# Spreading the modulation slabs of two later layers over both products of the second MLP

## The chip, the cores and the metric

One Trainium2 chip, one core of it. A time is the device time of one execution in microseconds (us), the median of several runs. The kernel before takes 2263.5 us (three runs: 2257.25, 2263.5 and 2268.2).

## The reference, cut to what matters

Four layers, each a token mixer (Hyena, gated linear attention, latent attention, Hyena) and then a squared-ReLU MLP, over 256 latent and 256 context tokens of width 1024. Every sub-layer is modulated by six vectors ("maps": shift, scale and gate, twice) that one linear map per layer makes from the condition vectors.

```python
for i in range(DEPTH):                       # 4 layers
    mod_l = split(silu(c)     @ ada_w[i] + ada_b[i], 6)     # six maps, latent tokens
    mod_c = split(silu(c_ctx) @ ada_w[i] + ada_b[i], 6)     # the same, context tokens
    x_lat = x_lat + mod_l[2] * mixer(modulate(rmsnorm(x_lat), mod_l[0], mod_l[1]))
    h = modulate(rmsnorm(x_lat), mod_l[3], mod_l[4])
    x_lat = x_lat + mod_l[5] * (square(relu(h @ mlp_w1[i])) @ mlp_w2[i])
    # the context tokens likewise, with mod_c, as long as a later layer reads them
```

`ada_w[i]` is 1024 x 6144 in f32, `mlp_w1[i]` 1024 x 4096, `mlp_w2[i]` 4096 x 1024. The maps of layers 2 and 3 depend on the condition vectors alone, so they can be made at any time before those layers.

## The kernel before, in words

Matrix products run on TensorE (PE) as three passes of a split operand: weights and activations are each cut into a high and a low part, and `mm3` (L369 to L371) multiplies high by high, high by low and low by high. A weight tile of 512 KB is loaded by SyncE's DMA queue (SP) into `wraw` (5 buffers), rounded by ScalarE (ACT) into `wh` (L359, 4 buffers), and GpSimd (POOL) makes the rest `wl` (L360, 4 buffers).

**The second MLP** (`mlp`, layer 1, 512 tokens) is the place of the change. `hidden(c)` makes 128 hidden units for all tokens: 24 matmuls of 512 columns into a bank `mm` (two banks; `cv` for two of the first four), then on ACT the ReLU (L645), on VectorE (DVE) the square (L646), on ACT the high part `fH` (L176) and on DVE the low part `fL` (L177). There are 32 of them. `residual` is the second product: for each group of four hidden blocks, 8 output tiles, each 12 matmuls of 512 columns into one of three `cv` banks, and after each tile two DVE additions into `x` (L600, one per 256 tokens). A `cv` bank is free for the next tile when these two are done. The loop over 8 groups makes the first hidden block of the next group, then the 8 tiles of this group, then the other three hidden blocks of the next group.

**The maps of layers 2 and 3** are made beside this MLP, by the generator `ada_lone`. There are 12 maps, each of 8 slabs of `ada_w` (128 x 1024, 512 KB, tag `adaw`, three buffers, named `lw` here), so 96 slabs, loaded on the same SP queue as the weights. DVE multiplies a slab by one element of the condition vector per partition and adds: two instructions of 128 x 512 per slab into two PSUM tiles `st` (L434 for the first slab, L436 after). Two of the 12 maps (layer 2, q = 0 and 1, third and fourth in order) are also wanted for the context tokens and take a third instruction of 128 x 1024 per slab into an SBUF tile `la` (L440, L442). After the eighth slab the sums over the partitions follow: four or eight small matmuls with ones on PE (L449, into the bank `ada`), a 32 x 32 transpose on DVE (L388) and the bias (L391, L394) in `ada_part`.

**What sets the order.** A scheduler orders each engine's instructions by priority of the program's order and by its own times; each engine then runs its list in that order. `more()` lets slabs out after each of 28 hidden blocks, at 96/26 = 3.69 slabs a block and none in the tiles; `issue_after(behind())` lets a slab's DVE work issue only after the low part of the latest hidden block (`last[0]`). The last slab of a map and its sums over the partitions are one step of the generator.

Of the kernel before, what the change touches and what calls it, by code (L numbers as in the profile page):

```python
# [15 lines left out]
ALU = mybir.AluOpType  # L16
# [4 lines left out]
KD = D // P  # L21
# [106 lines left out]
def trunk_kernel(ctx: ExitStack, tc: tile.TileContext, ins: dict, table, zpos, out, layers=(0, 1, 2, 3)):  # L128
    nc = tc.nc
# [11 lines left out]
    def nm(s):  # L141
        seq[0] += 1
        return f"{s}_{seq[0]}"
# [5 lines left out]
    def bank(tag="mm"):  # L149
        if tag in turns:  # L150

            turns[tag] += 1
            if turns[tag] % (banks[tag] + 1) == 0:
                tag = "ada"
        return pp.tile([P, 512], F32, tag=tag, name=nm(tag), bufs=banks[tag])
# [85 lines left out]
    def scratch(n, shape, dt=F32):  # L241
        return up.tile(shape, dt, tag=f"uL{n}", name=nm("scr"))
# [3 lines left out]
    for b in range(8):  # L246
        src = g["x"] if b < 4 else g["ctx"]
        t = up.tile([P, 512], F32, tag=f"uH{b}", name=nm("xr"))
        r0, c0 = (b % 4) // 2 * P, b % 2 * 512
# [37 lines left out]
    if need_hy:  # L287
# [10 lines left out]
        for q, w in enumerate((w1, w2)):  # L298
            ps = bank()
# [6 lines left out]
        ps = bank()  # L306
# [7 lines left out]
        r = scratch(1, [P, 2, SEQ], F32R)  # L314
# [9 lines left out]
    xT = [cp.tile([P, TOK], F32, tag=f"x{k}", name=f"x{k}") for k in range(KD)]  # L324
    for k in range(KD):
        ps = bank("cv")
# [41 lines left out]
    def mm3(ps, lh, ll, rh, rl, start, stop):  # L368
        nc.tensor.matmul(ps, lh, rh, start=start, stop=False)  # L369
        nc.tensor.matmul(ps, lh, rl, start=False, stop=False)  # L370
        nc.tensor.matmul(ps, ll, rh, start=False, stop=stop)  # L371


    mods = {}
# [8 lines left out]
    def ada_part(i, q, ps, s):  # L383

        m, a = ada_maps(i)
        n = s.stop - s.start
        tr = np_.tile([P, KD, 32], F32, tag="adatr", name=nm("adatr"), bufs=1)
        nc.vector.transpose(tr.rearrange("p t c -> p (t c)"), ps)  # L388
        o = pcol[("ada_b", 0 if i < 2 else 2)] + (i % 2) * 48 + q * KD
        bias = params[:, o : o + KD].unsqueeze(2).broadcast_to([P, KD, n])  # L390
        nc.vector.tensor_tensor(m[:, q, :, s], tr[:, :, :n], bias, ALU.add)  # L391
        if q in (1, 4):
            gn = pcs("norm1_g" if q == 1 else "norm2_g", i * KD, KD).unsqueeze(2).broadcast_to([P, KD, n])
            nc.vector.scalar_tensor_tensor(a[:, q // 4, :, s], m[:, q, :, s], 1.0, gn, ALU.add, ALU.mult)  # L394
# [22 lines left out]
    def ada_lone(parts, mp, behind):  # L417

        hd = D // 2
        for i, q, n in parts:

            run = [bank("st") for _ in range(2)]
            acc = [mp.tile([P, D], F32, tag=f"la{r}", name=nm("la"), bufs=1) for r in range(n)]
            for k in range(KD):
                wt = wp.tile([P, D], F32, tag="adaw", name=nm("lw"), bufs=3)
                nc.sync.dma_start(wt, g["ada_w"][i, k * P : (k + 1) * P, q * D : (q + 1) * D])
                with tc.issue_after(behind()):
                    for b in range(2):  # L430
                        cols = slice(b * hd, (b + 1) * hd)
                        dst = acc[0][:, cols] if k == KD - 1 else run[b]
                        if k == 0:
                            nc.vector.tensor_scalar(dst, wt[:, cols], sT[:, k, 0:1], None, ALU.mult)  # L434
                        else:
                            nc.vector.scalar_tensor_tensor(dst, wt[:, cols], sT[:, k, 0:1], run[b], ALU.mult, ALU.add)  # L436
                    for r in range(1, n):
                        c = sT[:, k, r : r + 1]
                        if k == 0:
                            nc.vector.tensor_scalar(acc[r], wt, c, None, ALU.mult)  # L440
                        else:
                            nc.vector.scalar_tensor_tensor(acc[r], wt, c, acc[r], ALU.mult, ALU.add)  # L442
                if k < KD - 1:
                    yield
            ps = bank("ada")
            for r in range(n):
                av = acc[r].rearrange("p (t j c) -> p j t c", j=4, c=32)
                for j in range(4):
                    nc.tensor.matmul(ps[32 * j : 32 * j + 32, r * 256 : (r + 1) * 256], ones[:, :32], av[:, j],  # L449
                                     start=True, stop=True, tile_position=(0, 32 * j))  # L450
            for r in range(n):
                ada_part(i, q, ps[:, r * 256 : (r + 1) * 256], slice(r, r + 1) if n == 2 else slice(0, 2))
            yield

    ada_q = []

# [3 lines left out]
    def pump(n, keep=0):  # L460

        while n > 0 and ada_q and ada_q[0][1] > ada_q[0][2][keep]:
            next(ada_q[0][0], None)
            ada_q[0][1] -= 1
            n -= 1
            if ada_q[0][1] == 0:
                next(ada_q.pop(0)[0], None)
# [110 lines left out]
                mm3(ps[:, s], wh[:, k, :m], wl[:, k, :m], uH[k][:, s], uL[k][:, s],  # L578
                    k == 0 and n == 0, k == KD - 1 and n == len(parts) - 1)

    def residual(i, gi, wmat, r0, fH, fL, nt, tag="mm", halves=False):

        nk = len(fH)
        parts = [slice(r * SEQ, (r + 1) * SEQ) for r in range(nt // SEQ)] if halves else [slice(0, nt)]

        def slabs(c):
            return [wload(wmat[r0 + p * 2 * P : r0 + (p + 1) * 2 * P, c * 512 : (c + 1) * 512]
                          .rearrange("(k p) c -> p k c", p=P), [P, 2, 512]) for p in range(nk // 2)]

        def columns(c, w, s):  # L590
            for d in range(4):
                ps = bank(tag)
                for k in range(nk):
                    wh, wl = w[k // 2]
                    mm3(ps[:, s], wh[:, k % 2, d * P : (d + 1) * P], wl[:, k % 2, d * P : (d + 1) * P],
                        fH[k][:, s], fL[k][:, s], k == 0, k == nk - 1)
                dt = c * 4 + d
                for r in range(s.start // SEQ, s.stop // SEQ):
                    q = slice(r * SEQ, (r + 1) * SEQ)
                    nc.vector.scalar_tensor_tensor(xT[dt][:, q], ps[:, q], mods[i][:, gi, dt, r : r + 1],  # L600
                                                   xT[dt][:, q], ALU.mult, ALU.add)

        if nk == 2 or halves:
            w = [slabs(0), slabs(1)]
            for s in parts:
                if s.start > 0:
                    last_part.append(tc.cur_priority)
                for c in range(2):
                    columns(c, w[c], s)
        else:  # L610
            for c in range(2):
                columns(c, slabs(c), parts[0])


    def mlp(i, nt, later=None, lone=()):
# [3 lines left out]
        with ExitStack() as es:  # L619
# [3 lines left out]
            if later is not None:  # L623
                fp = es.enter_context(tc.tile_pool(name=nm("fs"), bufs=1))
                later = filters(later, fp, dft_table(fp, "dftt", fp, "w4r"), "st", True)
            last = [None]
            extra = ada_lone(lone, mp, lambda: last[0])

            def hidden(c):
# [23 lines left out]
            groups = HID // 512  # L653
# [23 lines left out]
                                                               ALU.mult, ALU.add)  # L677

            fs = [hidden(c) for c in range(4)]
            count = [0]  # L680

            def more():
                count[0] += KD * len(lone)
                while count[0] >= 4 * groups - 6:
                    count[0] -= 4 * groups - 6
                    next(extra, None)

            for grp in range(groups):
                if later is not None:
                    for _ in range(2 if grp == 0 else 1):  # L690
                        next(later, None)

                nxt = []
                if grp + 1 < groups:
                    nxt.append(hidden(4 * grp + 4))
                    more()
                if single:
                    accumulate(grp)
                else:
                    residual(i, 5, g["mlp_w2"][i], grp * 512, [f[0] for f in fs], [f[1] for f in fs], nt, "cv",  # L700
                             halves=grp == groups - 1)
                if grp + 1 < groups:
                    for q in range(1, 4):
                        nxt.append(hidden(4 * grp + 4 + q))
                        more()
                        pump(1, 16)
                fs = nxt
                pump(2, 16)

    def together(chains):  # L710

        while chains:
            chains = [c for c in chains if next(c, chains) is not chains]
# [762 lines left out]
    lone = []  # L1476
    if len(layers) == DEPTH:
        lone = [(2, q, 2 if q < 2 else 1) for q in (3, 4, 0, 1, 2, 5)] + [(3, q, 1) for q in range(6)]
# [5 lines left out]
    for li, i in enumerate(layers):  # L1484
        kind, j = i % 3, i // 3
        both = any(l % 3 != 0 for l in layers[li + 1 :])
        nt = TOK if both else SEQ
# [71 lines left out]
```

## Time and profile before

| | before |
|---|---|
| median of three runs | 2263.5 us (2257.25 to 2268.2) |
| profiled execution | 2267.3 us, its span 2265.5 us |
| PE busy, share of the span | 2096.4 us, 93% |
| DVE busy | 1345.5 us, 59% |
| POOL busy | 1118.0 us, 49% |
| ACT busy | 905.7 us, 40% |
| DMA, mean | 145 GB/s |

PE is the engine with the most work, and for most of the span its line in the profile's 40 slices is at 9 (90% or more busy). The slices of the second MLP are those from about 1140 to 1510 us; several of them show PE at 8 or 7 and the DMA share at its highest since the start. Matmuls are pipelined: a matmul's shown duration is longer than its share of the engine's time, so the pitch from one start to the next is what counts.

### The profile page before, as it was taken

What the parts mean: (1) busy time and instruction counts of PE and PEld (TensorE: products, weight loads), DVE (VectorE), ACT (ScalarE), POOL (GpSimd) and SP (SyncE); (2) the same over time, 40 slices, a digit from 0 to 9 for tenths busy, and PEclk for the clock granted to TensorE, in tenths of its full rate; (3) what the DMA queues carried; (4) which work ended last, traced back from release to release, by engine and by line L of the source; (5) the groups of instructions that cost most, each with busy time, mean ns of one, the idle gap of its engine ahead of it and who ended that gap; (6) DMA issues with size and microseconds to landing.
All of it is one profiled execution on the core that took longest, in us unless ns stands there. A gap on an engine that the chain in (4) does not pass through costs nothing. (4 is left out here: it accounts for less than half of the span.)

```text
span 2265.5 us, 33310 instructions
## 1 busy us (share of the span) xinstructions
PE 2096.4 (93%) x12834; PEld 1781.8 (79%) x12834; DVE 1345.5 (59%) x2412; ACT 905.7 (40%) x1505; POOL 1118.0 (49%) x669
## 2 busy tenths in 40 slices
PE   6998999899999999998899988898989997887998
PEld 3766687777888889876777767687779997887998
DVE  7855887764344354455747976668673227996223
ACT  2642333343333234444432222236445445544444
POOL 5653444256544443322243333334347886674886
PEclk7998999999999999999999999999999997998999
DMA  9666635533333332212137677733135564433663
GB/s 313 185 211 222 206 112 177 167 96 117 110 105 99 107 88 74 67 57 65 47 117 246 211 253 227 244 115 109 66 116 164 180 190 131 126 115 94 182 191 112
DMA packets 322301, 329.12 MB, mean 145 GB/s; under 512 B 21276, under 2 KB 248673, under 8 KB 322143
## 3 DMA queue, kind: packets, MB, share of 16 engines
q1 hardware_dynamic: 321012, 326.05, 46.3%
q8 instruction: 101, 1.65, 0.3%
q10 hardware_dynamic: 587, 0.61, 0.1%
q14 instruction: 57, 0.47, 0.1%
q0 software_dynamic: 544, 0.34, 0.1%
HBM read 317.51 MB, written 9.44 MB: 144 GB/s over the span
## 5 line engine op out<-in xcount | busy, mean ns | idle before, releaser
L360 POOL TENSOR_TENSOR wl<-wraw,wh 128x1024 fp32r<-128x1024 f32 (+2 forms) x378 | 908.0, 2416 | 944.9 <-ACT wh L359 887.4
L359 ACT CAST wh<-wraw 128x1024 fp32r<-128x1024 f32 (+2 forms) x378 | 390.3, 1041 | 615.7 <-PE mm L370 229.4
L370 PE MATMUL mm<-uL,wh 128*128 128x512 f32 (+3 forms) x1288 | 455.1, 354 | 14.1 <-DVE uL L531 8.7
L369 PE MATMUL mm<-uH,wh 128*128 128x512 f32 (+3 forms) x1288 | 454.0, 356 | 14.5 <-DVE zb L568 5.4
L371 PE MATMUL mm<-uH,wl 128*128 128x512 f32 (+3 forms) x1288 | 451.5, 352 | 0.0
L369 PEld LDWEIGHTS mm<-uH,wh 128*128 128x128 f32 (+1 forms) x1288 | 249.6, 195 | 56.6 <-issue 15.1
L370 PEld LDWEIGHTS mm<-uL,wh 128*128 128x128 f32 (+1 forms) x1288 | 251.0, 195 | 49.3 <-DVE uL L531 13.1
L371 PEld LDWEIGHTS mm<-uH,wl 128*128 128x128 f32 (+1 forms) x1288 | 251.3, 195 | 32.5 <-issue 3.0
L369 PE MATMUL cv<-fH,wh 128*128 128x512 f32 (+1 forms) x576 | 213.3, 377 | 28.6 <-DVE x L600 21.3
L370 PE MATMUL cv<-fL,wh 128*128 128x512 f32 (+1 forms) x576 | 213.5, 373 | 0.7 <-DVE fL L177 0.6
L371 PE MATMUL cv<-fH,wl 128*128 128x512 f32 (+1 forms) x576 | 212.4, 372 | 0.0
L600 DVE SCALAR_TENSOR_TENSOR x<-cv,mods,x 128x256 f32<-128x256 f32 x256 | 112.1, 477 | 114.0 <-PE cv L371 113.8
L369 PEld LDWEIGHTS cv<-fH,wh 128*128 128x128 f32 x576 | 110.4, 193 | 52.0 <-issue 25.1
L370 PE MATMUL sum<-fL,wh 128*128 128x256 f32 x512 | 138.5, 278 | 0.0
L369 PE MATMUL sum<-fH,wh 128*128 128x256 f32 x512 | 137.0, 278 | 0.0
L371 PE MATMUL sum<-fH,wl 128*128 128x256 f32 x512 | 136.8, 278 | 0.0
L370 PEld LDWEIGHTS cv<-fL,wh 128*128 128x128 f32 x576 | 111.0, 193 | 20.4 <-issue 1.3
L371 PEld LDWEIGHTS cv<-fH,wl 128*128 128x128 f32 x576 | 110.5, 192 | 19.0 <-issue 0.7
L369 PE MATMUL mm<-oH,wh 128*128 128x256 f32 (+1 forms) x288 | 102.6, 358 | 23.5 <-DVE x L600 18.0
L646 DVE SCALAR_TENSOR_TENSOR mm<-mm,r 128x512 f32<-128x512 f32 x60 | 41.6, 694 | 130.1 <-ACT r L645 130.1
L436 DVE SCALAR_TENSOR_TENSOR st<-lw,sT,st 128x512 f32<-128x512 f32 x144 | 101.5, 747 | 22.3 <-DMA lw<-in_ada_w_dram 22.2
L565 DVE COPY rbias<-st 128x1 f32<-128x1 f32 x32 | 5.1, 158 | 163.5 <-PE st L371 163.5
(479 smaller groups left out, 4565.4 us busy)
## 6 DMA issues: line engine op xcount, KB each, us to landing
wraw<-in_mlp_w_dram SPq DMA_DIRECT2D x256, 512.0 KB
adaw<-in_ada_w_dram SPq DMA_DIRECT2D x96, 512.0 KB
lw<-in_ada_w_dram SPq DMA_DIRECT2D x96, 512.0 KB
wraw<-in_hy_w_in_dram SPq DMA_DIRECT2D x48, 512.0 KB
wraw<-in_gla_w_in_dram SPq DMA_DIRECT2D x24, 512.0 KB
spec<-S SPq DMA_DIRECT2D x16, 512.0 KB
wraw<-in_hy_w_out_dram SPq DMA_DIRECT2D x16, 512.0 KB
S<-spec SPq DMA_DIRECT2D x32, 256.0 KB
```

What stands on the lines that cost most here:

```text
L359: nc.scalar.copy(wh[r0:r1, :n], raw[r0:r1, :n])
L360: nc.gpsimd.tensor_tensor(wl[r0:r1, :n], raw[r0:r1, :n], rounded(wh[r0:r1, :n]), ALU.subtract)
L369: nc.tensor.matmul(ps, lh, rh, start=start, stop=False)
L370: nc.tensor.matmul(ps, lh, rl, start=False, stop=False)
L371: nc.tensor.matmul(ps, ll, rh, start=False, stop=stop)
L436: nc.vector.scalar_tensor_tensor(dst, wt[:, cols], sT[:, k, 0:1], run[b], ALU.mult, ALU.add)
L565: nc.vector.tensor_copy(bias, ps[:, SEQ : SEQ + 1])
L600: nc.vector.scalar_tensor_tensor(xT[dt][:, q], ps[:, q], mods[i][:, gi, dt, r : r + 1], xT[dt][:, q], ALU.mult, ALU.add)
L646: nc.vector.scalar_tensor_tensor(r, r, 0.0, pos, ALU.max, ALU.mult)
```

## The change

Slabs are let out after every piece of matmul work in proportion to its matmuls: `more(24)` after a hidden block, and `more(12)` after each tile of `residual` in the first seven groups, through the new argument `each`. With `total` = 7 x (4 x 24 + 8 x 12) - 24 = 1320, a hidden block lets out 96 x 24/1320 = 1.745 slabs and a tile 0.873. After a tile, `last[0]` is the tile's second addition, so the slab's DVE work is put behind that. The generator now yields after every slab, the eighth too, and the sums over the partitions of a map are made at the start of its next step, which then goes on to the first slab of the next map; a last loop finishes the twelfth map. The computation is the same.

```diff
@@ ada_lone, end of the loop over the slabs
-                if k < KD - 1:
-                    yield
+                yield
+
             ps = bank("ada")
...
                 ada_part(i, q, ps[:, r * 256 : (r + 1) * 256], slice(r, r + 1) if n == 2 else slice(0, 2))
-            yield
@@ residual
-                    nc.vector.scalar_tensor_tensor(xT[dt][:, q], ps[:, q], mods[i][:, gi, dt, r : r + 1],
-                                                   xT[dt][:, q], ALU.mult, ALU.add)
+                    add = nc.vector.scalar_tensor_tensor(xT[dt][:, q], ps[:, q], mods[i][:, gi, dt, r : r + 1],
+                                                         xT[dt][:, q], ALU.mult, ALU.add)
+                if each is not None:
+                    each(add.ins)
@@ mlp
-            count = [0]
-
-            def more():
-                count[0] += KD * len(lone)
-                while count[0] >= 4 * groups - 6:
-                    count[0] -= 4 * groups - 6
+
+            total, count = (groups - 1) * (4 * 24 + 8 * 12) - 24, [0]
+
+            def more(matmuls):
+                count[0] += KD * len(lone) * matmuls
+                while count[0] >= total:
+                    count[0] -= total
                     next(extra, None)
+
+            def after_tile(ins):
+                last[0] = ins
+                more(12)
...
-                    more()
+                    more(24)
...
                     residual(i, 5, g["mlp_w2"][i], grp * 512, [f[0] for f in fs], [f[1] for f in fs], nt, "cv",
-                             halves=grp == groups - 1)
+                             halves=grp == groups - 1,
+                             each=after_tile if lone and grp + 1 < groups else None)
...
-                        more()
+                        more(24)
...
+            for _ in extra:
+                pass
```

**How the order moves, place 1.** DVE in the sixth group, from the end of the middle one of three hidden blocks in a row to the first tile's addition (`mm` and `fL` belong to a hidden block, `lw`, `st` and `la` to a map, `cv` and `x` to a tile). Before:

```order
L436 SCALAR_TENSOR_TENSOR st_12002<-lw_12062,sT,st_12002 128x512
L177 TENSOR_TENSOR fL_12101<-mm_12073,fH_12100 128x512
L436 SCALAR_TENSOR_TENSOR st_12001<-lw_12104,sT,st_12001 128x512
L436 SCALAR_TENSOR_TENSOR st_12002<-lw_12104,sT,st_12002 128x512
L436 SCALAR_TENSOR_TENSOR la_12003<-lw_12108,sT,st_12001 128x512
L436 SCALAR_TENSOR_TENSOR la_12003<-lw_12108,sT,st_12002 128x512
L646 SCALAR_TENSOR_TENSOR mm_12134<-mm_12134,r_12133 128x512
L434 TENSOR_SCALAR st_12120<-lw_12123,sT 128x512
L434 TENSOR_SCALAR st_12121<-lw_12123,sT 128x512
L177 TENSOR_TENSOR fL_12162<-mm_12134,fH_12161 128x512
L600 SCALAR_TENSOR_TENSOR x_179<-cv_12193,mods_5225,x_179 128x256 x2
```

The same place of the change (L648 is L646 of before):

```order
L177 TENSOR_TENSOR fL_12093<-mm_12065,fH_12092 128x512
L436 SCALAR_TENSOR_TENSOR st_12001<-lw_12096,sT,st_12001 128x512
L436 SCALAR_TENSOR_TENSOR st_12002<-lw_12096,sT,st_12002 128x512
L648 SCALAR_TENSOR_TENSOR mm_12107<-mm_12107,r_12106 128x512
L177 TENSOR_TENSOR fL_12135<-mm_12107,fH_12134 128x512
L436 SCALAR_TENSOR_TENSOR st_12001<-lw_12138,sT,st_12001 128x512
L436 SCALAR_TENSOR_TENSOR st_12002<-lw_12138,sT,st_12002 128x512
L600 SCALAR_TENSOR_TENSOR x_179<-cv_12158,mods_5225,x_179 128x256 x2
L600 SCALAR_TENSOR_TENSOR x_180<-cv_12177,mods_5225,x_180 128x256 x2
L436 SCALAR_TENSOR_TENSOR st_12001<-lw_12142,sT,st_12001 128x512
L436 SCALAR_TENSOR_TENSOR st_12002<-lw_12142,sT,st_12002 128x512
```

One slab instead of two or more stands between two hidden blocks, and the slabs go on between the tiles' additions.

**Place 2.** DVE among the tiles of the second group, where the first map with a third instruction (`la` of 128 x 1024) runs, in the change:

```order
L600 SCALAR_TENSOR_TENSOR x_183<-cv_10739,mods_5225,x_183 128x256 x2
L442 SCALAR_TENSOR_TENSOR la_10681<-lw_10702,sT,la_10681 128x1024
L434 TENSOR_SCALAR st_10679<-lw_10682,sT 128x512
L436 SCALAR_TENSOR_TENSOR st_10678<-lw_10702,sT,st_10678 128x512
L600 SCALAR_TENSOR_TENSOR x_184<-cv_10759,mods_5225,x_184 128x256 x2
L442 SCALAR_TENSOR_TENSOR la_10681<-lw_10722,sT,la_10681 128x1024
L436 SCALAR_TENSOR_TENSOR st_10679<-lw_10702,sT,st_10679 128x512
L436 SCALAR_TENSOR_TENSOR st_10678<-lw_10722,sT,st_10678 128x512
L388 STREAM_TRANSPOSE adatr_10674<-ada_10669 128x256
L442 SCALAR_TENSOR_TENSOR la_10681<-lw_10754,sT,la_10681 128x1024
L600 SCALAR_TENSOR_TENSOR x_185<-cv_10774,mods_5225,x_185 128x256 x2
```

Before, one L442 stood between two additions here, and the next six came behind hidden blocks.

**Place 3.** The SP queue at the start of the second group (`wraw` is a weight, `lw` a slab). Before:

```order
L358 DMA wraw_10650<-in_mlp_w_dram 128x2x512
L428 DMA lw_10448<-in_ada_w_dram 128x1024
L428 DMA lw_10452<-in_ada_w_dram 128x1024
L428 DMA lw_10456<-in_ada_w_dram 128x1024
L358 DMA wraw_10656<-in_mlp_w_dram 128x2x512
L358 DMA wraw_10722<-in_mlp_w_dram 128x2x512
L358 DMA wraw_10728<-in_mlp_w_dram 128x2x512
L358 DMA wraw_10794<-in_mlp_w_dram 128x8x128
L358 DMA wraw_10852<-in_mlp_w_dram 128x8x128
L428 DMA lw_10460<-in_ada_w_dram 128x1024
```

And in the change:

```order
L358 DMA wraw_10623<-in_mlp_w_dram 128x2x512
L428 DMA lw_10323<-in_ada_w_dram 128x1024
L428 DMA lw_10342<-in_ada_w_dram 128x1024
L428 DMA lw_10373<-in_ada_w_dram 128x1024
L428 DMA lw_10407<-in_ada_w_dram 128x1024
L358 DMA wraw_10629<-in_mlp_w_dram 128x2x512
L428 DMA lw_10426<-in_ada_w_dram 128x1024
L358 DMA wraw_10727<-in_mlp_w_dram 128x2x512
L428 DMA lw_10481<-in_ada_w_dram 128x1024
L428 DMA lw_10485<-in_ada_w_dram 128x1024
L358 DMA wraw_10733<-in_mlp_w_dram 128x2x512
```

The slab loads now stand between the weight loads of the tiles too, one or two behind each. Everything ahead of the second MLP's first tile stands in the same order as before; behind this MLP the lists differ in a few short stretches of the last layer.

## Rows read from the trace of the kernel before

**Rows 1.** Busy time of each engine from the first slab to the last.

```profile
1160.00:1508.00 348.00, 319.68 (x1437) 254.90 (x1440) 246.52 (x403) 86.05 (x108) 130.54 (x57) 0.96 0.69 222
```

**Rows 2.** PE's timeline: idle of over 1 us between 1160 and 1508.

```profile
1211.82 0.47 PE L369 MATMUL cv<-fH,wh 128*128 128x512 f32 x1 [3.21 <-DVE x L600]
...
1261.64 0.77 PE L369 MATMUL cv<-fH,wh 128*128 128x512 f32 x1 [3.46 <-DVE x L600]
...
1310.86 0.64 PE L449 MATMUL ada<-la,ones 128*32 128x256 f32 x8 [1.13 <-DVE la L436]
1316.58 0.76 PE L369 MATMUL cv<-fH,wh 128*128 128x512 f32 x1 [5.09 <-DVE x L600]
...
1370.78 0.77 PE L369 MATMUL cv<-fH,wh 128*128 128x512 f32 x1 [5.93 <-DVE x L600]
...
1421.24 0.47 PE L369 MATMUL cv<-fH,wh 128*128 128x512 f32 x1 [3.62 <-DVE x L600]
...
1472.10 1.08 PE L449 MATMUL ada<-la,ones 128*32 128x256 f32 x8 [4.65 <-DVE la L436]
```

**Rows 3.** PE's timeline behind the stalls at 1316 and 1370.

```profile
1317.14 0.63 PE L370 MATMUL cv<-fL,wh 128*128 128x512 f32 x1
...
1322.26 0.60 PE L370 MATMUL cv<-fL,wh 128*128 128x512 f32 x1
...
1323.18 0.39 PE L370 MATMUL cv<-fL,wh 128*128 128x512 f32 x1
...
1327.52 0.39 PE L371 MATMUL cv<-fH,wl 128*128 128x512 f32 x1
...
1373.48 0.59 PE L369 MATMUL cv<-fH,wh 128*128 128x512 f32 x1
```

**Rows 4.** A window of 2 us there; third number from the end: granted clock.

```profile
1318.00:1320.00 2.00, 2.00 (x6) 1.61 (x5) 2.00 (x5) 0.87 (x1) 0.00 (x0) 0.50 0.48 197
```

**Rows 5.** DVE's timeline ahead of the stall that ends at 1472.

```profile
1463.16 2.72 DVE L436 SCALAR_TENSOR_TENSOR st<-lw,sT,st 128x512 f32<-128x512 f32 x4
1467.38 0.76 DVE L436 SCALAR_TENSOR_TENSOR st<-lw,sT,st 128x512 f32<-128x512 f32 x1 [1.50 <-DMA lw<-in_ada_w_dram]
...
1471.22 0.73 DVE L436 SCALAR_TENSOR_TENSOR la<-lw,sT,st 128x512 f32<-128x512 f32 x1
1471.87 1.65 DVE L600 SCALAR_TENSOR_TENSOR x<-cv,mods,x 128x256 f32<-128x256 f32 x4
```

**Rows 6.** DVE's timeline in tiles without slabs.

```profile
1169.77 0.88 DVE L600 SCALAR_TENSOR_TENSOR x<-cv,mods,x 128x256 f32<-128x256 f32 x2 [1.84 <-PE cv L371]
1172.49 0.88 DVE L600 SCALAR_TENSOR_TENSOR x<-cv,mods,x 128x256 f32<-128x256 f32 x2 [1.84 <-PE cv L371]
```

**Rows 7.** Instructions by line and shape, 1155 to 1510: count, busy, mean ns, idle before.

```profile
L360 POOL TENSOR_TENSOR wl<-wraw,wh 128x1024 fp32r<-128x1024 f32 x56 | 134.3, 2408 | 221.3 <-ACT wh L359 209.5 <-DMA lw<-in_ada_w_dram 11.8
L436 DVE SCALAR_TENSOR_TENSOR st<-lw,sT,st 128x512 f32<-128x512 f32 x144 | 101.5, 747 | 22.3 <-DMA lw<-in_ada_w_dram 22.2
...
L442 DVE SCALAR_TENSOR_TENSOR la<-lw,sT,la 128x1024 f32<-128x1024 f32 x14 | 26.7, 1904 | 0.0
L646 DVE SCALAR_TENSOR_TENSOR mm<-mm,r 128x512 f32<-128x512 f32 x28 | 19.4, 692 | 33.7 <-ACT r L645 33.7
L177 DVE TENSOR_TENSOR fL<-mm,fH 128x512 fp32r<-128x512 f32 x28 | 19.1, 683 | 5.2 <-ACT fH L176 5.2
```

**Rows 8.** DVE's timeline at the first hidden blocks with slabs.

```profile
1186.73 4.04 DVE L436 SCALAR_TENSOR_TENSOR st<-lw,sT,st 128x512 f32<-128x512 f32 x6
...
1193.37 1.42 DVE L436 SCALAR_TENSOR_TENSOR st<-lw,sT,st 128x512 f32<-128x512 f32 x2 [2.00 <-DMA lw<-in_ada_w_dram]
```

**Rows 9.** SP's timeline there.

```profile
1188.16 2.96 SPq L428 DMA_DIRECT2D lw<-in_ada_w_dram  x3
```

**Rows 10.** The third instruction by its line: duration min/median/max in ns.

```profile
L442 DVE SCALAR_TENSOR_TENSOR la<-lw,sT,la x14: 1266/1302/3494, 1220.1 to 1291.0; 128x1024 f32<-128x1024 f32 x14
```

**Rows 11.** What the SP queue waited for, 1150 to 1510: total, times, longest.

```profile
SPq L358 <- POOL wl L360: 126.0, 40, 10.1
```

More of the change, by code (lines that the diff above doesn't have):

```diff
@@ L579, in gemm_T, with residual @@
                     k == 0 and n == 0, k == KD - 1 and n == len(parts) - 1)
-    def residual(i, gi, wmat, r0, fH, fL, nt, tag="mm", halves=False):
+    def residual(i, gi, wmat, r0, fH, fL, nt, tag="mm", halves=False, each=None):
         nk = len(fH)
```

## The prediction

> **What bounds the kernel now.** The page names PE as the engine with most work, so I look for PE's idle time where the slabs run. The windows view says how much there is: from the first slab to the last, 348 us, PE is busy for 319.7 us and DVE for 246.5 us, at a mean granted clock of 0.96 [rows 1]. PE's timeline shows where the idle lies: seven waits of over 1 us, all for DVE, five of them for an addition of a tile (L600) that frees a `cv` bank and two for the last sum of a map (`la`) [rows 2]. They add up to 3.21 + 3.46 + 1.13 + 5.09 + 5.93 + 3.62 + 4.65 = 27.1 us. Six of the seven groups with slabs have one such spot, at the same place: the fourth tile, behind three hidden blocks in a row.
>
> Each stop but the one of 3.21 us is followed by matmuls at half clock. Behind the stop at 1316 there are 14, 0.427 us from start to start ((1322.26 - 1317.14)/12), where the full clock gives 0.228 us ((1327.52 - 1323.18)/19) [rows 3]; the granted clock there is 0.50, the lower of the two levels [rows 4]. Behind 1370 there are seven, from 1370.78 to 1373.48 [rows 2, 3], and behind 1261, 1421 and 1472 as many. So 14 + 4 x 7 = 42 matmuls lose 0.2 us each: 8.3 us. **Idle and clock together: 35.4 us.** That is all that the change can win here.
>
> Why DVE is late is read in two steps. First its work: a slab costs 4.04/3 = 1.35 us [rows 8], and a hidden block's square and low part 0.69 + 0.68 = 1.38 us [rows 7]. A block lets out 3.69 slabs, so DVE has 3.69 x 1.35 + 1.38 = 6.4 us to do for each block, and PE needs 24 x 0.228 = 5.5 us. Then the loads: a slab that SP issued at 1188.16 [rows 9] held DVE until 1193.37 [rows 8], 5.2 us. Its buffer is then in use for 1.35 us, and three buffers give one slab per (5.2 + 1.35)/3 = 2.2 us; a block's 3.69 slabs need 8.1 us, again more than 5.5 us. Both lags pile up over the blocks, and the additions stand behind the slabs in DVE's list. The stop that ends at 1472 shows it: four slab instructions, a wait of 1.50 us for a load, more slabs, and only then four L600, done together [rows 5]. In tiles without slabs nothing is late: the additions come every 2.72 us and DVE waits 1.84 us before each pair of 0.88 us [rows 6].
>
> **The change part by part.** Nothing is added or removed: the 96 slab loads, their DVE instructions, the small matmuls, transposes and bias additions are the same. They move.
>
> *The spread, maps with one column (80 slabs).* A hidden block now lets out 1.745 slabs: 1.745 x 1.35 + 1.38 = 3.7 us of DVE against 5.5 us of PE. A tile lets out 0.873: 0.873 x 1.35 + 0.88 = 2.1 us against 2.72 us. Loads at 2.2 us a slab need 3.8 us per block and 1.9 us per tile. Both fit, DVE with 1.8 us to spare in a block and 0.6 us in a tile. What covers a single late slab is the three `cv` banks: an addition may be two tiles (5.4 us) late before PE stops. Without that cover a late load would cost its wait: 1.50 and 2.00 us in the two rows shown [rows 5, 8].
>
> *The spread, maps with two columns (16 slabs).* Here a slab also has L442, at least 1.27 us [rows 10], so 2.62 us. A block needs 1.745 x 2.62 + 1.38 = 5.95 us (0.48 over PE's time), a tile 0.873 x 2.62 + 0.88 = 3.17 us (0.45 over). A group holds 4 x 1.745 + 8 x 0.873 = 13.96 slabs, so the 16 last for 1.15 groups and DVE falls behind by 1.15 x (4 x 0.48 + 8 x 0.45) = 6.3 us. L442 also ran longer than its minimum: 26.7 - 14 x 1.27 = 8.9 us in all [rows 7]. The lag of 15.2 us less the cover of 5.4 us leaves 9.8 us of idle at most, and nothing if the lag is caught up in between. I take about 7 us of idle in two stops, each with seven matmuls at half clock (1.4 us): **10 us left over**. I stay near the upper end since the slabs with L442 are now denser among the tiles.
>
> L442 is slow beside POOL: its median is 1.30 us and its longest 3.49 us [rows 10], and POOL's `wl` takes 2.41 us [rows 7] and fills 130.5 of 348 us [rows 1]. The Trainium skill ("SBUF — State Buffer", section "Who interferes with whom") says that a VectorE instruction with two SBUF inputs and a GpSimd instruction that reads SBUF exclude each other for a whole instruction; by that each of the 14 could wait for 2.41 us, 33.7 us where the rows have 8.9 us, and 25 us more would be left over.
>
> *The sums over the partitions.* They come one step later, so DVE's list has the eighth slab's instructions done before PE reaches L449. Two of the seven stops were waits for such a sum, 1.13 and 4.65 us [rows 2], counted above. Between a gain of those 5.8 us and a loss of the same I take the gain, since the late slab was the cause in both. The next map's first slab is behind the transpose only where the order puts it there; 0 us.
>
> *The SP queue.* Slab loads now stand between the tiles' weight loads too, and SP stands still at weight loads until POOL has freed a buffer: 126.0 us in 40 waits, 3.15 us each [rows 11]. What stands behind is a slab; what covers it is the third buffer. I count 0, and a rival below prices it.
>
> *The end of the MLP and the later layers.* The last slabs stand before the last block's square as they did; the lists behind differ in few places. 0 us, with 2 us either way for the range.
>
> Sum: 35.4 - 10 = 25.4 us off. The profiled execution took 2267.3 us, so 2241.9 us; it lies 3.8 us above the median of the three runs, so I forecast **2238 us**.
>
> **The rivals.**
>
> *Nothing is left over.* The list keeps L442 behind the additions and the cover holds: the whole 35.4 us, 2267.3 - 35.4 - 3.8 = 2228 us. For it: the order mixes L442 and additions one by one. Against it: the 15 us of lag. Chance 0.18.
>
> *The loads pace the tiles.* If every slab also pays SP's 3.15 us, a buffer's round is 9.7 us, 3.2 us a slab, and the tiles ask for one every 2.72/0.873 = 3.1 us. The additions then wait behind a late slab, and the stops move from the fourth tile into the tiles. With one such wait of 3.15 us past the cover in each of seven groups, 22 us come back, without half clock (the stop of 3.21 us had none): 2267.3 - 35.4 + 22 - 3.8 = 2250 us. Against it: most weight waits fall while the buffers are full anyway. Chance 0.2.
>
> *The sums stop PE (slower).* L449 stands in PE's own list with no bank as cover, in the middle of hidden blocks and tiles. If the last slab of each map were late, each of 12 sums would stop PE as at 1472: 4.65 us and seven matmuls at half clock, 6.05 us, 72.6 us in all: 2267.3 - 35.4 + 72.6 - 3.8 = 2301 us. It decides from 35.4/12 = 3 us per map on. Two of 12 waited before, and with DVE not behind there is no reason for more. Chance 0.05.
>
> *L442 blocked each time.* If each third instruction starts just behind a `wl` and stands still for its whole 2.41 us [rows 7], that is 14 x 2.41 = 33.7 us; DVE falls behind by 6.3 + 33.7 - 5.4 = 34.6 us and the win is gone: 2263 us. This is the case by the Trainium skill's "SBUF — State Buffer". The rows bear out the block, but for about half of the instructions only (the median is the minimum but for 0.04 us [rows 10]). Chance 0.05.
>
> **How the numbers follow.** The forecast has 0.5, and 0.02 is left for the later layers' order. A measurement of this kernel can tell some 0.5% from no change: below 2252 us is faster. The forecast and the first rival lie there, and of the second some 0.12 of its 0.2: 0.8. The rest of the second, the fourth and the remainder are no change: 0.14. Slower keeps 0.06. The range reaches from 2223 (the first rival, with the lowest run 6 us below the median) to 2256 (the second rival with 2 us of the later layers and the spread of runs).
>
> **What would show it.** Right: PE's timeline between 1160 and about 1480 has no wait for L600 at the fourth tile of the groups with one-column maps; the matmuls at 0.43 us fall from 42 to 14 or fewer; what idle is left lies in the second to fourth groups, behind L442; DVE waits for `lw` stay under 22 us and do not release PE; the stretch from first slab to last is some 25 us shorter. Wrong: waits of PE for additions spread over the tiles with a slab's DMA wait just before (loads), PE waiting at L449 for `la` in more than two maps (sums), or L442 at a mean well above 1.9 us (port).

## The result and the profile after

The changed kernel takes **2227.8 us** (median of 4 runs, 2226.46 to 2229.64), the kernel before 2265.6 us beside it (4 runs, 2257.25 to 2268.2): a ratio of **0.984**, 95% interval 0.982 to 0.986. It is faster by 37.8 us. The forecast of 2238 us stood 10 us too high; the result lies inside its range. The time is that of the rival in which nothing is left over (2228 us).

The profiled execution took 2229.64 us, its span 2227.9 us, 37.6 us less than before. The first slab starts at 1159.42 us (before 1160.28) and the last ends at 1469.5 us (before 1506.5), so the stretch between them went from 346.2 to 310.1 us. Of the 37.6 us, 36.1 lie in it; 0.9 us lie ahead of it and 0.6 behind.

The page's first part of the changed kernel, busy time of each engine:

```profile
span 2227.9 us, 33311 instructions
PE 2081.7 (93%) x12834; PEld 1773.8 (80%) x12834; DVE 1339.7 (60%) x2412; ACT 907.9 (41%) x1505; POOL 1122.9 (50%) x669
```

Instructions are as many as before on every engine. PE's busy time fell by 14.7 us. Of these, 10.7 us lie between the first slab and the last, where a matmul at half clock had counted as busy for longer (0.63 us against 0.39 us in [rows 3]); the rest lies ahead of the slabs, where nothing was changed. The windows view of the stretch with slabs:

```profile
1160.00:1470.00 310.00, 307.07 (x1416) 245.75 (x1415) 243.09 (x401) 84.87 (x106) 133.64 (x56) 1.00 0.78 249
```

Against [rows 1], DVE's work is the same (243.09 and 246.52 us), and PE is idle for 2.9 of 310 us where it was for 28.3 of 348 us. The granted clock is 1.00 where it was 0.96. The same bytes come in less time: 249 GB/s, before 222.

What PE waited for, by line, in the stretch of the changed kernel (total, times, longest), then its one stop of over 1 us, and the matmuls behind it:

```profile
PE cv L369 <- DVE x L600: 2.6, 4, 1.7
```

```profile
1255.66 0.47 PE L369 MATMUL cv<-fH,wh 128*128 128x512 f32 x1 [1.67 <-DVE x L600]
1255.96 0.40 PE L370 MATMUL cv<-fL,wh 128*128 128x512 f32 x1
1256.20 0.40 PE L371 MATMUL cv<-fH,wl 128*128 128x512 f32 x1
1256.43 0.40 PE L369 MATMUL cv<-fH,wh 128*128 128x512 f32 x1
```

The stops of [rows 2] are gone but for this one, among the slabs of the two-column maps. No matmul waits for `la` at L449 any more. Behind the stop the matmuls soon start 0.23 us apart, the pitch at full clock in [rows 3].

DVE's instructions by line and shape in the stretch of the changed kernel (count, busy, mean ns, idle before):

```profile
L436 DVE SCALAR_TENSOR_TENSOR st<-lw,sT,st 128x512 f32<-128x512 f32 x144 | 101.7, 750 | 9.6 <-DMA lw<-in_ada_w_dram 9.6
L600 DVE SCALAR_TENSOR_TENSOR x<-cv,mods,x 128x256 f32<-128x256 f32 x117 | 51.0, 478 | 5.2 <-PE cv L371 5.2
L442 DVE SCALAR_TENSOR_TENSOR la<-lw,sT,la 128x1024 f32<-128x1024 f32 x14 | 23.1, 1649 | 1.0 <-DMA lw<-in_ada_w_dram 1.0
```

Against [rows 7] the wait for slabs ahead of L436 fell from 22.3 to 9.6 us; the price of an instruction is as it was. L442 takes 1649 ns in the mean where it took 1904: over its minimum of 1.27 us, 5.3 us in all, before 8.9 us. What the SP queue waited for:

```profile
SPq L358 <- POOL wl L360: 103.4, 47, 6.5
```

SP still stands at weight loads until POOL frees a buffer, for 103.4 us where it was 126.0 us [rows 11], and no stop of PE over 0.3 us in the groups with one-column maps comes of it.

### The profile page after: what moved, and what is told of

The parts are those of the page before. It is cut to its first block, busy times and chain, and to the rows that moved or that the text cites. A ratio compares the mean times of both kernels' runs of the same rounds, so it can differ in the third digit from the quotient of the medians.

```text
span 2227.9 us, 33311 instructions
## 1 busy us (share of the span) xinstructions
PE 2081.7 (93%) x12834; PEld 1773.8 (80%) x12834; DVE 1339.7 (60%) x2412; ACT 907.9 (41%) x1505; POOL 1122.9 (50%) x669
## 5 line engine op out<-in xcount | busy, mean ns | idle before, releaser
L370 PEld LDWEIGHTS mm<-uL,wh 128*128 128x128 f32 (+1 forms) x1288 | 250.5, 195 | 46.4 <-DVE uL L530 10.7
L600 DVE SCALAR_TENSOR_TENSOR x<-cv,mods,x 128x256 f32<-128x256 f32 x256 | 112.5, 479 | 83.9 <-PE cv L371 83.9
L648 DVE SCALAR_TENSOR_TENSOR mm<-mm,r 128x512 f32<-128x512 f32 x60 | 41.8, 696 | 136.7 <-ACT r L647 136.7
L436 DVE SCALAR_TENSOR_TENSOR st<-lw,sT,st 128x512 f32<-128x512 f32 x144 | 101.7, 750 | 9.6 <-DMA lw<-in_ada_w_dram 9.6
```

What stands on the lines that cost most here:

```text
L600: add = nc.vector.scalar_tensor_tensor(xT[dt][:, q], ps[:, q], mods[i][:, gi, dt, r : r + 1], xT[dt][:, q], ALU.mult, ALU.add)
L648: nc.vector.scalar_tensor_tensor(r, r, 0.0, pos, ALU.max, ALU.mult)
```

## Experiments

Three accounts stood at the start. By the forecast's, DVE was late in the hidden blocks by its work and by the slabs' loads, and the spread removed both. By its two rivals, the later sums had a share of their own, or the loads alone were the cause.

**1. The spread without the later sums.**

```diff
-                yield
-
+                if k < KD - 1:
+                    yield
             ps = bank("ada")
...
+            yield
```

> The changed kernel, with each map's sum over the partitions back behind its eighth slab as before. Theory (the spread alone took the idle away; the sums stopped PE before only because DVE was late): 2228 to 2231 us, as the changed kernel or up to 3 us behind it, no stop of PE over 1.5 us at L449. Rival (the sums' move has a share of its own): the two stops for la of 1.13 and 4.65 us come back with their half clock, 2234 us or more; if every map's sum then stops PE by 2 us or so, 2250 us.

Measured: 2226.6 us (2224.53 to 2231.63), ratio to before 0.9837 (0.9811 to 0.9862). PE's waits for DVE in the stretch, total, times and longest:

```profile
PE cv L369 <- DVE x L601: 2.7, 4, 1.7
PE cv L370 <- DVE fL L177: 0.6, 1, 0.6
PE cv L369 <- ACT fH L176: 0.6, 2, 0.4
```

No wait at L449: once DVE is in time, a sum stops nothing, whether early or late. The spread alone is the whole gain.

**2. The later sums without the spread.** The diff's other half: `yield` after the eighth slab too, the count of before, and the loop over `extra` at the end.

> The kernel before, with the sums over the partitions made one slab later and nothing spread. Theory: DVE is as late as before, so the five stops for L600 stay (21.3 us) and the matmuls at half clock with them; 2258 to 2266 us, at most 5.8 us + 1.4 us off. Rival (the sums have a share of their own): 2255 us or less, with the stops for L600 shorter as well.

Measured: 2261.3 us (2258.19 to 2269.31), ratio 0.9989 (0.9973 to 1.0005): no change that can be told from none. PE's waits:

```profile
PE cv L369 <- DVE x L599: 20.9, 5, 5.3
PE ada L449 <- DVE la L436: 4.0, 2, 3.6
```

The five stops for the addition are there (21.3 us before by [rows 2]), and two waits for `la` as well: the sum came one slab later in the order, and DVE was late there too.

**3. The order of before with six slab buffers.** The kernel before with one line changed:

```diff
-                wt = wp.tile([P, D], F32, tag="adaw", name=nm("lw"), bufs=3)
+                wt = mp.tile([P, D], F32, tag="lw", name=nm("lw"), bufs=6)
```

> The kernel before, with six buffers for the slabs in place of three. If DVE is late by its work alone (6.4 us against PE's 5.5 us per hidden block, 3.6 us over a group's four blocks), the loads cost nothing and the time stays at 2262 to 2266 us. If the loads' round makes the larger part of the lag (2.2 us a slab, 8.1 us a block), then six buffers leave only the 3.6 us per group, less than the 5.4 us that the cv banks cover: most of the 35 us goes, 2230 to 2242 us, and DVE's waits for lw fall from 31.8 us to under 10 us.

Measured: **2228.9 us** (2227.62 to 2229.39), ratio 0.9843 (0.9819 to 0.9867): as fast as the changed kernel, with nothing spread, and a little better than expected. DVE's slab line, and PE's waits for the addition:

```profile
L436 DVE SCALAR_TENSOR_TENSOR st<-lw,sT,st 128x512 f32<-128x512 f32 x144 | 100.3, 744 | 0.0
L600 DVE SCALAR_TENSOR_TENSOR x<-cv,mods,x 128x256 f32<-128x256 f32 x116 | 49.9, 474 | 31.8 <-PE cv L371 31.7
```

```profile
PE cv L369 <- DVE x L600: 4.0, 2, 3.1
```

DVE waits for no slab. It still waits 31.8 us for PE at the additions, as in the kernel before (34.6 us) and unlike the changed one (5.2 us): its work is as bunched as before, and PE stops for over 1 us once (3.1 us) where it stopped seven times. So in this kernel the work of a burst was covered but for that, and what stopped PE was the time in which DVE stood still for loads in the hidden blocks.

**4. The changed kernel with two slab buffers.** In `ada_lone` and in the first layers' `adaw`, 3 becomes 2.

> The changed kernel, with two slab buffers in place of three (for the maps of the first layers as well). If the loads take part in the pace: a slab then comes each (5.2 + 1.35)/2 = 3.3 us, where the tiles ask for one each 3.1 us; DVE's waits for lw grow from 15.3 us to 40 us or more, PE waits for L600 in the tiles, and the time is 2235 to 2260 us. If the loads have slack in the spread order (a load takes less than 5.2 us when it isn't asked for in bursts): within 3 us of 2228 us.

Measured: 2242.8 us (2239.41 to 2248.11), ratio 0.991 (0.9886 to 0.9933), some 15 us behind the changed kernel. DVE's waits for slabs:

```profile
DVE st L436 <- DMA lw<-in_ada_w_dram: 34.6, 34, 2.7
DVE la L436 <- DMA lw<-in_ada_w_dram: 5.7, 7, 1.7
DVE st L434 <- DMA lw<-in_ada_w_dram: 4.1, 6, 1.1
```

They are 44.4 us, from 15.3. PE's two stops, then the windows with them and that of the whole stretch:

```profile
1262.12 0.77 PE L369 MATMUL cv<-fH,wh 128*128 128x512 f32 x1 [3.73 <-DVE x L600]
...
1312.51 0.68 PE L369 MATMUL cv<-fH,wh 128*128 128x512 f32 x1 [1.68 <-DVE x L600]
```

```profile
1212.00:1276.00 64.00, 60.07 (x265) 47.08 (x264) 59.80 (x86) 14.74 (x18) 24.41 (x10) 0.95 0.68 214
1276.00:1320.00 44.00, 42.32 (x195) 33.25 (x194) 35.49 (x59) 12.74 (x16) 19.14 (x8) 0.96 0.74 238
...
1163.00:1483.00 320.00, 313.81 (x1431) 251.20 (x1431) 246.64 (x402) 86.17 (x108) 131.05 (x57) 0.98 0.76 243
```

Its profiled span is 10.5 us longer than the changed kernel's (2238.4 and 2227.9), and 9.5 us of that lie between the first slab and the last: 3.4 us are more waiting for L600 (6.0 and 2.6), the two stops are followed by 21 matmuls at half clock, 4.2 us, and 1.9 us I can't place. The rest of the way to 15 us lies ahead of the slabs, where the first layers lost a buffer too, or is the scatter of runs. So in the spread order three buffers are enough and two are not.

The first stop stands among the two-column maps (their L442 run from 1219.0 to 1282.7 us), where DVE is busy for 59.80 of 64 us; the second stands 30 us behind them, after four waits for slabs of 5.1 us in all. In both places an instruction of 8 elements per partition also held DVE (L391 for 1.88 us, L394 for 2.26 us; see the last section). In the other groups no stop is over 0.3 us. And in all PE is idle for 6.2 of the 320 us, in the kernel before for 28.3 of 348 us, though DVE waits longer for slabs here (44.4 us) than there (31.8 us). It counts where DVE waits: spread over blocks and tiles most of the waits are covered, bunched in the hidden blocks they were not.

**5. The control for the third.** The kernel before, its three buffers moved to the pool of this MLP (the same line, `bufs=3`).

> The kernel before with its three slab buffers in the pool of this MLP, under a tag of their own, as the six buffers were: the control for them. If the number of buffers did it: 2260 to 2270 us, and the five stops for L600. If the place of the buffers had a share (fewer other loads that take them in turn): below 2255 us.

Measured: 2260.7 us (2256.83 to 2269.82), ratio 0.9985 (0.9968 to 1.0001). PE waits for L600 as before:

```profile
PE cv L369 <- DVE x L600: 18.3, 5, 5.0
PE ada L449 <- DVE la L436: 4.9, 3, 3.7
```

It was the number of buffers, not their place.

**6. One buffer more.** The order of before with `bufs=4`.

> The kernel before with four slab buffers in this MLP's pool. With the round of 6.55 us four buffers give a slab per 1.64 us, 6.0 us per hidden block against PE's 5.5 us: 0.5 us late per block, 2.2 us per group, under the cover. So nearly all of the gain comes with one buffer more: 2228 to 2238 us. If the round grows with more loads under way (the DMA engines being the limit), half or less of it: 2245 us or more.

Measured: 2239.4 us (2229.05 to 2242.28), ratio 0.9883 (0.9863 to 0.9902). About 25 us of the gain come with one buffer, a little less than expected. PE's and DVE's waits:

```profile
DVE st L436 <- DMA lw<-in_ada_w_dram: 12.0, 9, 2.6
PE cv L369 <- DVE x L600: 9.3, 4, 5.2
```

From three to four to six buffers DVE's waits for slabs go 31.8, 12.0, 0 us and PE's for the addition 21.3, 9.3, 4.0 us: they fall together.

**7. Both.** The changed kernel with six buffers, its line changed as in the third.

> The changed kernel with six slab buffers. Theory (the spread and the buffers take away the same idle time): nothing is left to win but the one stop of 1.67 us; 2224 to 2229 us, DVE's waits for lw under 3 us. Rival (each takes away a part of its own, and what the buffers leave of 0.89 + 3.15 us is not what the spread leaves): over 4 us less than the changed kernel, 2223 us or less.

Measured: 2228.1 us (2224.4 to 2228.4), ratio 0.9827 (0.9812 to 0.9842): with the changed kernel's ratio inside its interval. The spread and the buffers take away the same idle time, the buffers by ending the waits and the spread by parting them. No version tried is faster than the changed kernel by more than the runs scatter.

**8. The tie to the addition.** In `after_tile` the line `last[0] = ins` is left out.

> The changed kernel without the tie of a tile's slab to that tile's addition (slabs are let out after tiles as well, but the list may put them behind the last hidden block's low part alone). If the spread itself is what keeps the additions in time: within 3 us of 2228 us, as DVE has 0.6 us to spare per tile and the cv banks cover 5.4 us. If the tie has a part: DVE's list has slabs ahead of the additions that PE waits for, its stops for L600 come to 10 us or more in all and the time to 2238 us or more.

Measured: 2227.1 us (2221.89 to 2231.71), ratio 0.9843 (0.9826 to 0.986). The tie has no part in the time that can be measured.

**9 to 12. The price of the two-column maps,** the forecast's term that failed. The number of maps with L442 is set in one line, `lone = [(2, q, 2 if q < 2 else 1) ...]`: none, four (q = 0, 1, 2, 5 of layer 2) or all twelve.

> The changed kernel with no two-column map: the 14 L442, the two L440 and two transposes are left out, and the second sequence takes the first one's vector in two maps of the MLA layer. It prices what the two-column maps still cost in the spread order. By the term on record 10 us: 2218 us. By the trace of the changed kernel (two stops of 1.67 and 0.39 us, no matmul at half clock) 2 us: 2224 to 2228 us.

Measured: 2224.7 us (2223.65 to 2227.91), ratio 0.9828 (0.981 to 0.9846). Two such maps cost 2227.8 - 2224.7 = 3 us in the spread order, not 10, and the ranges of the two kernels overlap. PE's idle time between the first slab and the last makes 2 us of it (2.9 and 0.9 us); PE's own sums for the second column are 16 small matmuls more, and at 1243.59 us in the changed kernel 16 of them take 1.07 us.

> The changed kernel with four two-column maps in place of two (the two more vectors are read by no later step). With all twelve, 6.9 groups cost 67 us more than the changed kernel; DVE's lag per group is 5.5 + 14 x 0.38 = 10.8 us, 74.6 us in all, so the cover took 7.4 us. If the cover is that one sum for the stretch, four maps (2.3 groups) lag by 24.8 us and cost 17 us: about 2245 us. If each group covers anew: about 2232 us, twice what two maps show. If the cost goes by the number of L442 (67/70 = 0.96 us each, 14 more): about 2241 us.

Measured: 2246.9 us (2239.48 to 2248.11), ratio 0.9916 (0.9899 to 0.9933). Four such maps cost 22 us where two cost 3. The time is nearest to that of a cover used up once (2245 us), but 2241 us, a price for each L442, lies inside the range of the runs too. PE's new stops, against the changed kernel's one of 1.67 us:

```profile
1296.21 0.50 PE L369 MATMUL mm<-uH,wh 128*128 128x512 f32 x1 [2.09 <-DVE fL L177]
...
1310.84 0.76 PE L369 MATMUL cv<-fH,wh 128*128 128x512 f32 x1 [2.14 <-DVE x L600]
1360.34 0.64 PE L449 MATMUL ada<-la,ones 128*32 128x256 f32 x8 [2.37 <-DVE la L436]
```

> The changed kernel with all twelve maps made for both columns: 80 more L442 (the extra modulation vectors are computed and no later step reads them). DVE then has 14 x 2.62 + 4 x 1.38 + 8 x 0.88 = 49.3 us of work per group where PE has 4 x 5.5 + 8 x 2.72 = 43.8 us, so it is the bound whatever the cover: 5.5 us a group, 6.9 groups, less the cover of 5.4 us: 33 us, 2261 us; with L442 0.38 us over its minimum each (5.3/14, the trace of the changed kernel) 30 us more, 2291 us. If the cover catches up lags of this size as it did with two such maps: under 2245 us. If POOL holds up each L442 for a whole wl: over 2400 us.

Measured: 2295.0 us (2293.0 to 2299.22), ratio 1.0132 (1.0113 to 1.0151), near the 2291 us with L442's excess. DVE in the stretch:

```profile
1160.00:1535.00 375.00, 330.28 (x1491) 258.37 (x1489) 357.45 (x494) 86.57 (x109) 149.63 (x57) 0.94 0.64 205
```

```profile
L442 DVE SCALAR_TENSOR_TENSOR la<-lw,sT,la 128x1024 f32<-128x1024 f32 x84 | 136.8, 1628 | 0.0
```

DVE is busy for 357 of 375 us: here it is the bound. Put together: by lag (10.8 us a group) twelve maps are 74.6 us late and cost 2295.0 - 2224.7 = 70 us, four are 24.8 us late and cost 22 us, two are 11.6 us late and cost 3 us. Of a large lag most is paid, and of a small one little.

How far this goes is told by the profiled executions. Up to the first slab, all kernels but the one with two buffers run the same instructions in the same order on PE, DVE, ACT and POOL, and yet that slab starts anywhere from 1151.6 us (the eighth run) to 1164.3 us (the fifth). Counted from the first slab to the end, two, four and twelve maps cost 0.4, 17.5 and 68.5 us over none, and the change gains 36.8 us. So the covered part of the lag can't be read closer than some 3 to 11 us. No run changes the number of `cv` banks, so that these are the cover is argued and not shown.

> The kernel before with six buffers and all twelve maps for both columns (the extra vectors are read by no later step): the burst order where loads are no limit and DVE's work is. If a burst costs what DVE is late in it, whatever it could do among the tiles: 3.69 x 2.62 + 1.38 = 11.0 us per hidden block against 5.5 us, 22 us a group, less 5.4 us of cover, in 6.9 groups 115 us: about 2340 us, 50 us or more behind the changed kernel with the same maps. If only DVE's sum of work counts (the lists shift until it fits): as that kernel within 10 us.

Measured: 2299.7 us (2296.95 to 2301.36), ratio 1.0146 (1.013 to 1.0161), 5 us behind the changed kernel with the same twelve maps and 40 us ahead of the 2340 us for a burst. That reasoning falls. From the first slab to the end the two take the same in the profiled executions, 1136.1 and 1136.5 us. What PE waited for in the stretch here, then for L600 in the changed kernel with the twelve maps, then a piece of DVE's timeline among the tiles here:

```profile
PE cv L369 <- DVE x L600: 21.6, 7, 5.6
PE ada L449 <- DVE la L436: 7.2, 3, 6.0
PE cv L370 <- DVE fL L177: 4.1, 3, 1.9
```

```profile
PE cv L369 <- DVE x L600: 23.2, 5, 7.2
```

```profile
1221.69 0.86 DVE L600 SCALAR_TENSOR_TENSOR x<-cv,mods,x 128x256 f32<-128x256 f32 x2
1222.48 1.27 DVE L442 SCALAR_TENSOR_TENSOR la<-lw,sT,la 128x1024 f32<-128x1024 f32 x1
1223.67 0.74 DVE L436 SCALAR_TENSOR_TENSOR st<-lw,sT,st 128x512 f32<-128x512 f32 x1
1224.33 0.86 DVE L600 SCALAR_TENSOR_TENSOR x<-cv,mods,x 128x256 f32<-128x256 f32 x2
```

The waits for additions are of the size of the spread order's with the same maps, and the timeline shows why: the list of before, too, puts slabs between the additions. So a burst's work is caught up among the tiles, as long as the slabs are there.

## Why the prediction was right, and where it was off

**What bounds the kernel: right.** The 27.1 us of idle and 8.3 us at half clock were winnable, and they went. The stretch gave 36.1 us, 3.6 us more than the two less the 2.9 us that remain; 1.2 us of that are waits of under 1 us (28.3 us of idle by [rows 1] against the 27.1), the other 2.4 us I can't place.

**The cause: half right.** The prediction named two lags of DVE, work and loads. The third and the fifth run show that the loads decided: with DVE's work as bunched as ever, the stops but one are gone once slabs are there in time. The numbers of the prediction had it, had they been summed to the end: a group's four blocks are 4 x (6.4 - 5.5) = 3.6 us of work late, under the cover of 5.4 us, while the loads' 4 x (8.1 - 5.5) = 10.4 us are over it by 5 us, the size of the stops in [rows 2]. What it did not have is the fourth run's finding: the spread does not need the waits to go, only to be parted.

**The spread, one-column maps: right.** 0 us left over; no stop over 0.3 us, no matmul at half clock (42 before).

**The spread, two-column maps: the term that failed.** "10 us left over" was a lag of 6.3 + 8.9 us less the cover of 5.4, taken near its upper end. It measured 3 us (none against two such maps). L442 lost 5.3 us over its minimum, not 8.9, so the lag was 11.6 us; and over 8 of them were covered or caught up, not 5.4. That the lag does cost once it is larger, the runs with four and with twelve maps show. This term is 7 of the 10 us by which the forecast was off. The other 3: the profiled span fell by 5.1 us more than 35.4 less the 2.9 us that remain, and the profiled execution lies 1.8 us above the median of its runs where the forecast took off 3.8 us.

**The sums over the partitions: right in the outcome, wrong in the reason.** Their 5.8 us went, but by the spread; moving the sums alone leaves the time as it was and a wait of 3.6 us, and leaving them in place costs nothing.

**The SP queue, the end and the later layers: right.** 0 us counted; 0.6 us measured behind the stretch.

**The rivals.** "Nothing is left over" came true in the time, with a chance of 0.18: one stop of over 1 us is left. That the mixed order of L442 and additions is the reason, as it had it, no run shows by itself. "The loads pace the tiles" did not decide with three buffers (DVE waits 15.3 us for slabs, PE 2.6 us for additions); with two they made two stops, not one in each group. "The sums stop PE" had no case. "L442 blocked each time" would have needed 33.7 us; it lost 5.3 us.

## What to carry to other kernels

When an engine is late, split its lag into its own work and its waiting for data before choosing the cure: here one line that gives the slabs three more buffers is worth as much as the spread, and the two don't add. Compare each lag with the cover (banks, buffers) by itself, summed over the burst: here a lag of 11.6 us cost 3 us at most, and one of 74.6 us was paid nearly in full. Waits that are spread can be covered where the same waits in a bunch are not. And a term taken "near the upper end" needs a row that says why; it took the runs with none, four and twelve such maps to show that two of them lay below the edge.

## What had not been expected

The one stop left comes from an addition of 8 elements per partition. DVE's timeline of the changed kernel, then POOL's:

```profile
1251.22 1.24 DVE L442 SCALAR_TENSOR_TENSOR la<-lw,sT,la 128x1024 f32<-128x1024 f32 x1
1252.38 2.34 DVE L391 TENSOR_TENSOR mods<-adatr,params 128x8 f32<-128x8 f32 x1
1254.65 0.86 DVE L600 SCALAR_TENSOR_TENSOR x<-cv,mods,x 128x256 f32<-128x256 f32 x2
```

```profile
1251.35 3.35 POOL L360 TENSOR_TENSOR wl<-wraw,wh 128x1024 fp32r<-128x1024 f32 x1 [6.12 <-ACT wh L359]
```

L391 took 2.34 us, and ended as POOL's `wl` did (1254.72 and 1254.70 us); the same instruction took 0.16 us 4 us earlier (at 1248.27), with no `wl` beside it. The difference of 2.2 us is more than the stop of 1.67 us that PE had behind it. In the stretch two more L391 took 1.26 and 2.36 us and one L394 1.05 us, and each ended within 0.04 us of a `wl`; PE did not stop for them. The long L442 show the same: all ten of over 2 us in the two kernels ended some 1.08 us behind the end of a `wl`. The `wl` shown was itself 0.9 us longer than its usual 2.41 us [rows 7], and L442 ran beside its first 1.1 us. The Trainium skill ("SBUF — State Buffer", section "Who interferes with whom") calls the port pair that DVE and POOL share an exclusive lock. The rows agree with that, and in both directions. L436, which reads its sum from PSUM, shows no such thing in the same stretch: 726 to 760 ns over 144 instructions. So a tiny instruction could cost a whole `wl`; the prediction priced L442 alone for this.
